# Value sums in two fp32r passes over split pages, finer sample steps, and a new background order in a two-layer decoder step

## The chip, the cores and the metric

One core of a Trainium2 chip runs the whole kernel. The metric is device time in microseconds (us) of one execution. All inputs and outputs are fp32 in HBM.

The engines: TensorE (PE) multiplies, with weight loads shown apart (PEld); VectorE is DVE, ScalarE is ACT, GpSimd is POOL, and SyncE (SP) issues nearly all transfers. Each engine works through its own queue in order.

## The reference, cut to what matters

Two layers over two groups: a prompt (1 x 1024 tokens) and a sample (8 sequences x 8 new tokens behind a past of 1024 tokens in pages of 128). Layer 0 joins a convolution module with stick-breaking attention; layer 1 joins a short convolution with pooling; each is followed by a SwiGLU channel mixer. What the change touches is in layer 0:

```python
proj = hn @ w_in                       # a_val, a_gate, q, k, v
glu = a_val * sigmoid(a_gate)
a = silu(layer_norm(causal_depthwise_conv(ext, conv_w) + conv_b))   # width 31, 512 channels
# stick-breaking attention, 8 heads x 64:
z = einsum('nqhd,nkhd->nhqk', q, k) * scale + bias
log_1m = where(mask, log_sigmoid(-z), 0)
after = cumsum(log_1m, reverse=True) - log_1m
wgt = exp(where(mask, log_sigmoid(z) + after, -inf))
b = einsum('nhqk,nkhd->nqhd', wgt, v)
out = concatenate([a, b]) @ w_out
```

For the sample group k and v come from cache pages named by a page table (8 sequences x 8 pages), with 8 new rows behind them.

## The kernel before, in words

**Operands.** A large product splits weights and activations into a rounded part and a residual (fp32r) and runs three passes (`mm3`, L170). `w_split` (L152 on ACT, L153 on POOL) makes the two halves of a weight tile; three raw and three split tiles rotate. The foreground on PE is such blocks of 24 matmuls or more, one after the other, evacuated by DVE (L226, L230) from two or three accumulators.

**Foreground and background.** The foreground calls a slot function every two of a block's eight steps. In it `bg()` takes one more piece from a generator in `flow`, whose instructions so land between foreground matmuls. A `yield` ends a piece. What is left of a flow when the next stage needs its result is issued by `drain()` without foreground between.

- `flow_ab` runs during the combined input projection `in_proj` of the first half of the prompt (GA, 512 tokens) and of the rest with the sample (GB, 576): `conv_a` (31 taps, 26 of them on DVE with the sum in PSUM, five on ACT and POOL), `conv_norm(GA)`, `attention(GA)`.
- `flow_c` runs during the output projection and the channel mixer of GA: `attention(GB)`, then `conv_b` and `sample()` interleaved, then `conv_norm(GB)`. It is drained in `last_a`, the last out-blocks of the mixer.

**Prompt attention** works by units of one head and 128 queries in four steps, which overlap by one unit each: `s1` scores and two sigmoids (PE, ACT), `s2` scans and product (DVE), `s3` transposes of the weights and their copy `wt` (PE, ACT L826), `s4` value sum (PE L834, in fp32).

**The sample group.** `sample()` goes through 24 units (two sequences together, three key blocks), each in two steps `pr` of two head pairs. `load_k` fetches pages of 128 x 512 into `kst` (six buffers), `trans` transposes them on PE (L922) and splits them (ACT L925, DVE L926) into `kth`, `score` multiplies (L945). A step is three pieces: transposes of the next step's first pair, transposes of its second pair, scores. When two sequences have all scores, `weights`, `weights_b` and `weights_t` follow at fixed step distances (`chain`); `weights_t` transposes nine column blocks in one piece (L994) and copies them (L995). Then 16 value pages are queued in `pvq` and taken two a step: `pv` multiplies 64 weight columns with a page of 128 x 512 in fp32 (L1006), and after eight pages the new rows (L1012). `load_v` brings pages in pairs into two buffers. `conv_b` gets a piece at every second yield of value 2.

**in_proj** for GA starts with the block `first`, in whose middle `norm_a` is issued; `norm_b` (L218) follows the block, and behind it the evacuations.

## Time and profile before

| what | value |
| --- | --- |
| median of 3 runs | 2731.98 us (2730.38 to 2736.82) |
| profiled execution | 2730.78 us, span 2729.0 us |
| PE busy | 2612.9 us, 96% of the span |
| DVE, ACT, POOL busy | 1224.5, 860.4, 1035.5 us |
| HBM read and written | 198.09 and 18.69 MB |
| stage of prompt attention on GB | about 363 to 606 us |
| stage of conv_b and sample | about 606 to 1021 us |

A row of the costliest groups reads: line, engine, operation, tiles written and read, shapes, count, then busy time and mean duration in ns, then the idle time of the engine before such instructions and what ended it. A row of a timeline reads: start, duration, engine, line, operation, count, and in brackets the idle time before it with what ended that. Matmul durations overlap, so the price of one in a stream is the distance from start to start. A row of stretches reads: start and end, length, busy time with count of PE, weight loads, DVE, ACT and POOL, granted clock, DMA share and GB/s.

### The profile page before, as it was taken

The numbers are of one execution on the slowest core, as the hardware profiler recorded it, in microseconds if no ns is written. First come the engines' busy times: TensorE is split into PE (matmuls) and PEld (weight loads), VectorE is DVE, ScalarE is ACT, GpSimd is POOL, SyncE is SP. The second block draws the span as 40 slices with busy tenths as digits, with TensorE's granted clock in tenths as the row PEclk, the third lists the DMA queues.
The fourth block names the chain that finished last, engine by engine and source line by source line (L and its number), as shares of the span: only waits on it lengthen the run. The fifth ranks groups of instructions, "written<-read, shape, count | busy, mean of one in ns | idle before, by whom it ended". The sixth has DMA issues, their size and how long they took to land. (4 is left out here: it accounts for less than half of the span.)

```text
span 2729.0 us, 37771 instructions
## 1 busy us (share of the span) xinstructions
PE 2612.9 (96%) x15423; PEld 2370.5 (87%) x15423; DVE 1224.5 (45%) x1738; ACT 860.4 (32%) x1318; POOL 1035.5 (38%) x589
## 2 busy tenths in 40 slices
PE   7988999899999998899999999999999999999997
PEld 5787877777766656899999989999999999999997
DVE  3775767768777652332222243342222222222226
ACT  4435656653343323242222232123211111111112
POOL 5655233433333327454444452223322222222222
PEclk9999999999999998999999999999999999999999
DMA  6332241124445432422222231131111111111111
GB/s 199 108 102 62 60 114 47 54 64 147 133 132 148 125 116 62 151 78 86 79 85 85 86 99 39 39 100 51 46 44 47 47 40 46 47 43 43 47 39 66
DMA packets 293381, 218.75 MB, mean 80 GB/s; under 512 B 21506, under 2 KB 248962, under 8 KB 293193
## 3 DMA queue, kind: packets, MB, share of 16 engines
q1 hardware_dynamic: 293176, 216.33, 26.6%
q8 instruction: 122, 2.00, 0.3%
q14 instruction: 51, 0.41, 0.0%
q10 hardware_dynamic: 32, 0.01, 0.0%
HBM read 198.09 MB, written 18.69 MB: 79 GB/s over the span
## 5 line engine op out<-in xcount | busy, mean ns | idle before, releaser
L153 POOL TENSOR_TENSOR hl<-stage,hl 128x1024 fp32r<-128x1024 f32 x278 | 683.5, 2461 | 1204.6 <-ACT hl L152 790.0
L170 PE MATMUL acc<-x1t,hl 128*128 128x364 f32 (+1 forms) x4896 | 824.1, 330 | 7.1 <-DVE hb L230 6.4
L170 PEld LDWEIGHTS acc<-x1t,hl 128*128 128x128 f32 x4896 | 817.1, 189 | 9.2 <-ACT x1t L304 6.7
L170 PE MATMUL acc<-x,hl 128*128 128x288 f32 (+1 forms) x4704 | 809.3, 326 | 8.8 <-POOL hl L153 3.2
L170 PEld LDWEIGHTS acc<-x,hl 128*128 128x128 f32 x4704 | 688.2, 189 | 88.8 <-issue 36.0
L170 PE MATMUL acc<-hid,hl 128*128 128x364 f32 (+2 forms) x3024 | 534.5, 335 | 19.9 <-DVE hb L230 15.5
L170 PEld LDWEIGHTS acc<-hid,hl 128*128 128x128 f32 x3024 | 482.2, 191 | 58.5 <-DVE hb L230 20.9
L152 ACT ACTIVATE hl<-stage 128x1024 fp32r<-128x1024 f32 x278 | 291.9, 1053 | 584.3 <-PE acc L170 303.1
L226 DVE TENSOR_TENSOR tmp<-acc,rr 128x728 f32<-128x728 f32 (+2 forms) x230 | 160.8, 721 | 698.1 <-PE acc L170 697.2
L230 DVE TENSOR_TENSOR hb<-acc,hb 128x728 f32<-128x728 f32 (+2 forms) x368 | 255.6, 720 | 280.3 <-PE acc L170 278.9
L176 DVE TENSOR_TENSOR hid<-tmp,hid 128x512 fp32r<-128x512 f32 (+2 forms) x66 | 60.8, 921 | 200.7 <-ACT hid L175 200.7
L187 POOL TENSOR_TENSOR ss<-ss,tmp 128x512 f32<-128x512 f32 (+2 forms) x55 | 97.6, 1774 | 92.9 <-ACT tmp L186 91.9
L175 ACT ACTIVATE hid<-tmp 128x512 fp32r<-128x512 f32 (+2 forms) x66 | 53.5, 810 | 238.4 <-POOL tmp L378 238.3
L378 POOL TENSOR_TENSOR tmp<-tmp 128x512 f32<-128x512 f32 (+2 forms) x66 | 117.0, 1772 | 28.0 <-ACT tmp L366 27.9
L170 PE MATMUL acc<-x1a,hl 128*128 128x512 f32 x480 | 123.0, 410 | 3.4 <-POOL hl L153 2.3
L366 ACT ACTIVATE tmp<-tmp 128x576 f32<-128x576 f32 (+1 forms) x44 | 39.6, 900 | 256.1 <-DVE tmp L226 256.1
L170 PEld LDWEIGHTS acc<-x1a,hl 128*128 128x128 f32 x480 | 90.7, 193 | 27.2 <-POOL hl L153 3.8
L834 PE MATMUL o<-wt,vrow 128*64 128x128 f32 x576 | 78.1, 282 | 16.6 <-ACT wt L826 16.6
L834 PEld LDWEIGHTS o<-wt,vrow 128*64 128x64 f32 x576 | 62.5, 139 | 35.5 <-ACT wt L826 30.3
L688 DVE SCALAR_TENSOR_TENSOR cacc<-ext,par,cacc 128x512 f32<-128x512 f32 x120 | 90.1, 750 | 2.3
L364 POOL TENSOR_TENSOR tmp<-tmp 128x512 f32<-128x512 f32 x22 | 32.4, 1471 | 135.9 <-ACT tmp L363 125.1
L813 DVE TENSOR_TENSOR_SCAN q<-q,ones 128x384 f32<-128x384 f32 (+6 forms) x56 | 77.7, 1388 | 2.0
(222 smaller groups left out, 1898.0 us busy)
## 6 DMA issues: line engine op xcount, KB each, us to landing
stage<-in_w_ffn_in_dram SPq DMA_DIRECT2D x132, 512.0 KB
stage<-in_w_ffn_out_dram SPq DMA_DIRECT2D x66, 512.0 KB
stage<-in_w_in_even_dram SPq DMA_DIRECT2D x40, 512.0 KB
kst<-in_cache_k_dram SPq DMA_DIRECT2D x64, 256.0 KB
vst<-in_cache_v_dram SPq DMA_DIRECT2D x64, 256.0 KB
stage<-in_w_out_even_dram SPq DMA_DIRECT2D x16, 512.0 KB
stage<-in_w_in_odd_dram SPq DMA_DIRECT2D x16, 512.0 KB
park<-hb SPq DMA_DIRECT2D x16, 288.0 KB
```

The costliest lines, as they stand in the source:

```text
L152: act.activation(hl[:, 0], st, AF.Copy)
L153: pool.tensor_tensor(hl[:, 1], st, f32(hl[:, 0]), op=OP.subtract)
L170: pe.matmul(acc[:, b, :c1 - c0], w, x[:, xi, c0:c1], start=first and s == 0, stop=last and s == 2)
L175: act.activation(dst[:, 0], src, AF.Copy)
L176: dve.tensor_tensor(dst[:, 1], src, f32(dst[:, 0]), op=OP.subtract)
L187: pool.tensor_tensor(ss[:, g.cs], ss[:, g.cs], t[:, :g.n], op=OP.add)
L226: dve.tensor_tensor(d, a, r, op=OP.mult)
L230: dve.tensor_tensor(d, a, d, op=OP.add)
L378: pool.tensor_tensor(t[:, :n], t[:, :n], u[:, :n], op=OP.mult)
L688: dve.scalar_tensor_tensor(o, i, w, o, op0=OP.mult, op1=OP.add)
L813: dve.tensor_tensor_scan(e, e, ones[:, 0:1].to_broadcast([128, n - 128]), q[:, n - 128:n - 127], op0=OP.mult, op1=OP.mult)
L834: pe.matmul(o, vrow[h][:, j], w[:, j], start=j == 0, stop=j == i)
```

## The change

It does these things.

1. **Value sums** (`pv`, `weights_t`, `split_v`): each value page is split into rounded part (ACT) and residual (POOL), the weights likewise (ACT, DVE), with the two parts of the weights stacked as 128 columns. A page then is two fp32r matmuls of 128 x 512, and the sum has 128 rows, which `sel` adds up. Raw pages come one by one (`vst`, two buffers of one page); two split pages (`vhl`) are held.
2. **Keys**: transfers of half pages (128 x 256, eight buffers, five ahead); `kth` holds one head pair, in three buffers.
3. **Sample steps**: every piece is a step of its own; the order is transposes of the next step's first pair, scores of this step, transposes of the second pair. `weights_t` goes over three pieces. The distances in `chain` are now in pieces.
4. **Prompt attention**: `s3` comes ahead of `s2` and `s1`; three yields instead of one at the start; two `be` buffers instead of three.
5. **conv_a**: the add that joins the two partial sums is issued eight taps into the next channel; `a2` and `cacc` have two buffers; two yields at the end.
6. **conv_norm**: the scale and shift move from DVE to ACT.
7. **in_proj (GA)**: the second block is issued before `norm_b` and before the first block's evacuation. The first two blocks call no slot inside, the first none behind it either.

```diff
     def conv_a(ep, cp):
...
-            a2 = ep.tile([128, HALF], F, name="a2")
-            acc = cp.tile([128, 512], F, name="cacc")
+            a2 = ep.tile([128, HALF], F, name="a2", bufs=2)
+            acc = cp.tile([128, 512], F, name="cacc", bufs=2)
...
+                if j == OFF + 7 and last:
+                    last.pop()()
...
-            dve.tensor_tensor(a, acc, a2, op=OP.add)
+            last.append(lambda a=a, acc=acc, a2=a2: dve.tensor_tensor(a, acc, a2, op=OP.add))
+        yield 1
+        yield 1
+        last.pop()()
...
-                dve.tensor_scalar(y, y, pc(LNG + c - 1), pc(LNB + c - 1), op0=OP.mult, op1=OP.add)
+                act.activation(y, y, AF.Identity, scale=pc(LNG + c - 1), bias=pc(LNB + c - 1))
...
-                be = bt[u] = pa.tile([128, NKEY], F, name="be", bufs=3)
+                be = bt[u] = pa.tile([128, NKEY], F, name="be", bufs=2)
...
-            yield 1
+            for _ in range(3):
+                yield 1
             for u in range(len(units) + 3):
                 if u >= 3:
                     s4(u - 3)
+                if 2 <= u < len(units) + 2:
+                    s3(u - 2)
                 if 1 <= u < len(units) + 1:
                     s2(u - 1)
...
                     s1(u)
-                if 2 <= u < len(units) + 2:
-                    s3(u - 2)
...
-            KP = 6
+            KP = 5
...
+                    t = kst[j, pr] = sa.tile([128, 256], F, name="kst", bufs=KP + 3)
+                    page_to(t, cache_k[:, :, :, 4 * pr:4 * pr + 4], j)
...
+                    vst[i] = sa.tile([128, 512], F, name="vst", bufs=2)
+                    page_to(vst[i], cache_v, i)
+
+            def split_v(upto):
+                while len(vhl) + vdone[0] < min(upto, 64):
+                    i = len(vhl) + vdone[0]
+                    v = vst.pop(i)
+                    t = vhl[i] = sa.tile([128, 2, 512], FR, name="vhl", bufs=2)
+                    act.activation(t[:, 0], v, AF.Copy)
+                    pool.tensor_tensor(t[:, 1], v, f32(t[:, 0]), op=OP.subtract)
+                    load_v(i + 3)
...
+                t = kth[u, pr, i] = sa.tile([128, 2, 384], FR, name="kth", bufs=3)
...
+                wl = wts[bp] = sa.tile([128, 9, 2, 2, 64], FR, name="wl")
...
-                    act.activation(t[:, c0:c0 + n], m[:, :n * 128].rearrange("p (c r) -> p c r", r=128), AF.Copy)
+                    mv = m[:, :n * 128].rearrange("p (c b r) -> p c b r", b=2, r=64)
+                    o = wl[:, c0:c0 + n]
+                    act.activation(o[:, :, :, 0], mv, AF.Copy)
+                    dve.tensor_tensor(o[:, :, :, 1], mv, f32(o[:, :, :, 0]), op=OP.subtract)
+                    yield
...
-                load_v(i // 2 + 1)
-                pe.matmul(o, wts[bp][:, k, 64 * b2:64 * b2 + 64], vst[i // 2][:, k % 2], start=k == 0, stop=False)
-                if k % 2:
-                    vst.pop(i // 2)
-                    load_v(i // 2 + 3)
+                w = wts[bp][:, :, b2].rearrange("p c s r -> p c (s r)")
+                v = vhl.pop(i)
+                for s in range(2):
+                    pe.matmul(o, w[:, k], v[:, s], start=k == 0 and s == 0, stop=False)
+                vdone[0] += 1
+                split_v(i + 3)
                 if k < 7:
                     return
-                pe.matmul(o, wts[bp][:, 8, 64 * b2:64 * b2 + 64], vnew, start=False, stop=True)
+                for s in range(2):
+                    pe.matmul(o, w[:, 8], vn[:, s], start=False, stop=s == 1)
...
-            while s < len(steps) or chain or pvq or fins:
+            while s < 3 * len(steps) or chain or pvq or fins:
...
+                st, piece = divmod(s, 3)
+                if piece != 1 and st + 1 < len(steps):
+                    trans(*steps[st + 1], piece // 2)
+                if piece == 1 and st < len(steps):
+                    u, pr = steps[st]
                     bp, kb, b2 = units[u]
                     score(u, pr)
...
-                        for d, f in ((1, lambda w=w: next(w)), (2, lambda w=w: next(w)),
-                                     (3, lambda bp=bp: weights_b(bp)), (5, lambda bp=bp: weights_t(bp))):
+                        for d, f in ((2, lambda w=w: next(w)), (3, lambda w=w: next(w)),
+                                     (5, lambda bp=bp: weights_b(bp)), (8, lambda wt=wt: next(wt)),
+                                     (10, lambda wt=wt: next(wt)), (11, lambda wt=wt: next(wt))):
...
-                        chain.setdefault(s + 6, []).append(
+                        chain.setdefault(s + 13, []).append(
...
-                if pvq:
-                    pvq.pop(0)()
+                for _ in range(1 + (st >= len(steps))):
+                    if pvq and (piece != 1 or st >= len(steps)):
+                        pvq.pop(0)()
                 s += 1
-                yield 2
+                yield 1 if todo else 2
...
                 block(g, a, h, x, mid=lambda: box.setdefault("d", norm_a(g, ms, D)))
+                held_back = a
+                continue
+            elif i == first + 1 and first:
+                block(g, a, h, x)
                 norm_b(g, ms, box["d"])
+                evs[first](held_back)
                 evs[i](a)
```

More of the change, by code (lines that the diff above doesn't have):

```diff
@@ L631, in conv_a @@
     def conv_a(ep, cp):
-        g = GA
+        g, last = GA, []
         for c in range(4):
@@ L866, in sample @@
         units = [(bp, kb, b2) for bp in range(4) for kb in range(3) for b2 in range(2)]
-        kpages = [(2 * bp + b2) * 8 + 3 * kb + i for bp, kb, b2 in units for i in range((3, 3, 2)[kb])]
+        khalf = [((2 * bp + b2) * 8 + 3 * kb + i, pr) for bp, kb, b2 in units for pr in range(2)
+                 for i in range((3, 3, 2)[kb])]
         NK = 1032
@@ L914, in trans @@
                 j = (2 * bp + b2) * 8 + 3 * kb
[L915 to L929 removed]
+                load_k(khalf.index((j, pr)) + n)
+                t = kth[u, pr, i] = sa.tile([128, 2, 384], FR, name="kth", bufs=3)
+                m = ms()
+                hp = 2 * pr + i
+                for pg in range(n):
+                    pe.transpose(m[:, pg * 128:pg * 128 + 128], kst[j + pg, pr][:, i * 128:i * 128 + 128], ident)
+                act.activation(t[:, 0, :n * 128], m[:, :n * 128], AF.Copy)
+                dve.tensor_tensor(t[:, 1, :n * 128], m[:, :n * 128], f32(t[:, 0, :n * 128]), op=OP.subtract)
+                if i:
+                    load_k(khalf.index((j, pr)) + n + KP)
+                if kb == 2:
                     b = 2 * bp + b2
[L931 to L933 removed]
+                    new = knew[:, hp, 8 * b:8 * b + 8]
+                    act.activation(t[:, 0, 256:264], new, AF.Copy)
+                    dve.tensor_tensor(t[:, 1, 256:264], new, f32(t[:, 0, 256:264]), op=OP.subtract)
             def score(u, pr):
@@ L938, in score @@
                     z[u] = zp.tile([128, 512], F, name="z")
-                t = kth.pop((u, pr))
                 n = NB[kb]
@@ L942, in score @@
                     hp = 2 * pr + i
+                    t = kth.pop((u, pr, i))
                     q = qb[:, b2, hp * 128:hp * 128 + 128]
                     for s in range(2):
-                        pe.matmul(z[u][:, :n], q, t[:, s, i, :n], start=hp == 0 and s == 0, stop=hp == 3 and s == 1)
+                        pe.matmul(z[u][:, :n], q, t[:, s, :n], start=hp == 0 and s == 0, stop=hp == 3 and s == 1)
             def score_b(u):
@@ L963, in score_b @@
                     act.activation(qf[bp][:, o:o + n], zs[bp][:, :n], AF.Sigmoid, scale=-0.125, bias=brow[:, 1:2])
-            wx, wts, osum = {}, {}, {}
+            wts, osum = {}, {}
             def weights(bp):
@@ L1032, in sample @@
             fill_q(0)
-            load_v(2)
             for _ in range(6):
                 yield 1
+            split(vn, vnew)
+            split_v(1)
+            split_v(2)
             for i in range(2):
```

74 lines of the change are left out of this document (21 added, 53 removed).

## The prediction

> **What bounds the kernel now.** I read the page first, then the profiled execution by stretches, the timeline of TensorE (PE) for its gaps, and the timelines of the engines that end them.
>
> ```profile
> span 2729.0 us, 37771 instructions
> PE 2612.9 (96%) x15423; PEld 2370.5 (87%) x15423; DVE 1224.5 (45%) x1738; ACT 860.4 (32%) x1318; POOL 1035.5 (38%) x589
> 237.00:600.00 363.00, 335.79 (x2042) 280.71 (x2043) 268.43 (x287) 226.52 (x413) 118.77 (x115) 0.98 0.23 64
> 616.00:715.00 99.00, 91.35 (x448) 74.36 (x447) 83.16 (x147) 38.99 (x80) 38.93 (x20) 0.97 0.46 140
> 625.00:1020.00 395.00, 376.21 (x1607) 256.35 (x1605) 283.82 (x502) 139.84 (x286) 125.31 (x65) 0.98 0.44 132
> ```
>
> The last three rows are stretches: start:end, length, then busy time of PE, weight loads, DVE, ACT, POOL. PE has 116 us of idle time in 2729; so the time changes by PE work saved or added and by PE gaps closed or opened. Everything the diff touches lies before about 1100 us. The second cover is thin: in 616 to 715 us DVE is busy 83 of 99 us.
>
> The profiled execution took 2730.78 us (span 2729.0), 1.2 us under the median of the runs, so I carry differences over unchanged.
>
> **Value sums in the steady part (-26.7).**
>
> ```profile
> 732.03 1.07 PE L1006 MATMUL o<-vst,wts 128*64 128x512 f32 x2
> 733.03 1.66 PE L170 MATMUL acc<-hid,hl 128*128 128x512 f32 x6
> 734.53 0.86 PE L945 MATMUL z<-kth,qb 128*128 128x384 f32 x4
> 735.32 1.07 PE L1006 MATMUL o<-vst,wts 128*64 128x512 f32 x2
> 759.42 1.02 PE L1012 MATMUL o<-vnew,wts 128*64 128x512 f32 x2
> 760.37 1.66 PE L170 MATMUL acc<-x,hl 128*128 128x512 f32 x6
> ```
>
> Durations overlap, so I price from start to start. One fp32 page costs 1.00 us (732.03 to 733.03), recorded as two matmuls. Six fp32r matmuls of 512 columns take 1.50 (733.03 to 734.53), 0.25 each, which is one slot of the foreground between two background pieces. The new pv issues two such matmuls: 0.50. Bounds: 0.50 by this row and 1.00 if it gained nothing; I take 0.50, the same type and columns. 48 pages lie in the steady part: 48 x 0.50 = 24.0. The new rows cost 0.95 (759.42 to 760.37), now 0.50: 6 x 0.45 = 2.7. The last 16 pages come below.
>
> **Gaps that the reordering closes.**
>
> ```profile
> 41.94 2.05 PE L218 MATMUL m<-tmp,ones 128*128 128x512 f32 x2 [5.14 <-DVE tmp L209]
> 42.99 10.61 PE L170 MATMUL acc<-x1a,hl 128*128 128x512 f32 x36
> 161.66 1.09 PE L601 MATMUL m<-ident,tmp 128*128 128x128 f32 x4 [6.17 <-DVE tmp L226]
> 237.19 0.50 PE L796 MATMUL z<-kt,qa 128*128 128x512 f32 x1 [3.82 <-ACT qa L778]
> 239.94 0.76 PE L796 MATMUL z<-kt,qz 128*128 128x512 f32 x1 [2.25 <-POOL qz L762]
> 371.47 0.47 PE L796 MATMUL z<-kt,qa 128*128 128x512 f32 x1 [1.50 <-DVE kt L776]
> 372.79 0.47 PE L796 MATMUL z<-kt,qz 128*128 128x512 f32 x1 [0.84 <-DVE qz L779]
> L834 PE MATMUL o<-wt,vrow 128*64 128x128 f32 x576 | 78.1, 282 | 16.6 <-ACT wt L826 16.6
> L825 PE MATMUL m<-ident,be 128*128 128x128 f32 x288 | 42.0, 273 | 0.2 <-DVE be L815 0.2
> 722.11 0.33 PE L994 MATMUL m<-ident,wx 128*128 128x128 f32 x1 [1.83 <-ACT wts L995]
> 815.93 0.33 PE L994 MATMUL m<-ident,wx 128*128 128x128 f32 x1 [2.47 <-ACT wts L995]
> 909.29 0.33 PE L994 MATMUL m<-ident,wx 128*128 128x128 f32 x1 [1.83 <-ACT wts L995]
> 984.18 1.09 PE L994 MATMUL m<-ident,bet 128*128 128x128 f32 x8 [1.94 <-DVE bet L980]
> ```
>
> In in_proj the second block (24 matmuls, 6.0 us) now stands before norm_b and covers the 5.14. The 36 matmuls after that gap take 10.5 us against 36 x 0.25 = 9.0, a slow clock after idling: another 1.5. Together **-6.6**. Two accumulators wait instead of one, of three, so the next block still has one. What is late next is the evacuation after norm_b, with a whole block before its buffer is asked for.
>
> That edit costs four background slots (one of the first block, three of the second), so the convolution starts a block later and leaves less DVE backlog at 161.66. The backlog grows by what eight taps and an evacuation exceed one foreground block, under 1 us: **-0.9** (0 to -2). The deferred add of conv_a stays on DVE and only moves.
>
> Attention on the first half yields three slots instead of one. PE asked for z at 233.4 (237.19 less 3.82) and had both operands at 239.9, 6.1 us of gaps; two more slots (12 matmuls of 288 columns, by scale of the 0.25 some 1.7 us each) cover 3.5 of it: **-3.5** (-6.1 if ACT's Identity, which takes the DVE step out of the chain before it, brings POOL forward; -2 if POOL is simply full). On the second half two slots of 1.5 cover 1.50 and 0.84: **-2.3**.
>
> Moving s3 ahead takes the wt copies out from behind the two sigmoids on ACT and gives them two slots in the second half. The 16.6 us is the whole stake. Against it, the transposes now come sooner after DVE's product: one slot and one s1 earlier, about 2.5 us. They wait 0.2 us in all now, but DVE is busy 268 of 363 us there, and the shorter time leaves several units near zero. Bounds 0 and -16.6; I take two thirds: **-11**.
>
> weights_t in three slots removes the copy that PE waits for inside one piece: 8.07 us in the four rows. Left over is a transpose bank whose DVE subtraction queues behind two taps, about 0.5 us a group: **-6**.
>
> Whether the background still fits is a count of yields in the code. The first flow needed 113 of 121 slots; it now needs 117 of 117 (four lost, two more for conv_a, two for attention) and just fits. The second needed 269 of 280 and now needs 281 (the sample's tail 20 instead of 14, four more for conv_b, two for attention). So the last norm work is issued in the last slot, against the final out-blocks: **+2** (-2 to +8).
>
> **What the change newly asks for.** First the keys:
>
> ```profile
> 685.73 0.38 PE L922 MATMUL m<-ident,kst 128*128 128x128 f32 x2
> 691.47 0.41 DVE L926 TENSOR_TENSOR kth<-m,kth 128x256 fp32r<-128x256 f32 x1
> 694.28 0.66 PE L945 MATMUL z<-kth,qb 128*128 128x264 f32 x4
> L688 DVE SCALAR_TENSOR_TENSOR hb<-ext,par,hb x120: 279/285/2314, 648.8 to 1001.2; 128x64 f32<-128x64 f32 x120
> L688 DVE SCALAR_TENSOR_TENSOR hb<-ext,par,hb 128x64 f32<-128x64 f32 x120 | 57.4, 479 | 3.0
> ```
>
> A score used to follow its transposes by four slots (685.7 to 694.3); now by two, some 4.0 us. Here DVE finishes its residual at 691.9, 6.2 us after: a wait of about 2. This happens where no value pages run and DVE is full, 616 to 715 us; later, with PE slower per step, DVE keeps up. I put **+8** (0 to +15: half of the 16 steps there at 2). On DVE the 120 small taps take 479 ns on average against a median of 285: 23 us lost to something. POOL is busy 125 of 395 us there; 64 more subtractions of about 1.3 us add 83, so by scale 15 us more on DVE, most of it where DVE has room.
>
> The Trainium skill, page "SBUF — State Buffer", section "SBUF: two separate sides", names the cause: VectorE operations with two SBUF inputs and GpSimd operations that read SBUF lock one another out for the whole instruction. The rule speaks against moving splits to POOL. The row agrees (279 at least, 2314 at most).
>
> The half pages double the key transfers on SP, but five half pages lie ahead, so I cost them at nothing; if that cover went, each transfer would show as a PE wait at L922.
>
> Now the value pages. Each goes DMA, ACT copy, POOL subtraction, PE, in two raw and two split buffers; the next load into a raw buffer waits for POOL.
>
> ```profile
> L175 ACT ACTIVATE hid<-tmp 128x512 fp32r<-128x512 f32 x22 | 13.8, 629 | 44.6 <-POOL tmp L378 44.5
> L647 POOL TENSOR_TENSOR a<-a,tapb 128x512 f32<-128x512 f32 x16 | 20.7, 1296 | 0.5
> 988.49 1.99 PE L1006 MATMUL o<-vst,wts 128*64 128x512 f32 x4
> 990.40 1.66 PE L170 MATMUL acc<-hid,hl 128*128 128x512 f32 x6
> 992.00 1.93 PE L1006 MATMUL o<-vst,wts 128*64 128x512 f32 x4
> 991.09 11.24 SPq L419 DMA_DIRECT2D vst<-in_cache_v_dram  x8
> 1007.49 4.08 SPq L419 DMA_DIRECT2D vst<-in_cache_v_dram  x4
> 1011.83 1.93 PE L1006 MATMUL o<-vst,wts 128*64 128x512 f32 x4 [0.62 <-DMA vst<-in_cache_v_dram]
> 0.75 1.83 SPq L489 DMA_DIRECT2D xt<-in_x_prompt_dram  x4
> 3.92 0.47 PE L523 MATMUL m<-ident,xt 128*128 128x128 f32 x1
> ```
>
> A cycle of one buffer: copy 0.63, subtraction 1.30, release to issue 0.7 (990.40 to 991.09), transfer 4.3 (1007.49 to 1011.83) or at most 3.2 (0.75 to 3.92, the same 256 KB); I take 3.6, between, since the tail has few transfers beside it. That is **6.2 us for two pages** (5.8 to 7.0). A steady step asks for two pages every three slots: 4.5 + 0.7 for six transposes (under 685.73's 0.38 for two, as durations overlap) + 0.8 scores (734.53 to 735.32) + 1.0 = 7.0 us. It fits, barely. ACT waits at the split for a landing; queued behind it are the key copies, the gate's copies and the next weight split, and PE would meet that as late keys or weights. SP waits for POOL with the next weights behind it, which are due two blocks later.
>
> In the tail, the last 16 pages come two to a slot. PE alone would need 1.5 + 1.0 = 2.5 us a slot, before it took 3.5 (988.49 to 992.00), or 27.7 for eight. With two slots out of the buffers and six at the cycle: 2 x 2.5 + 6 x 6.2 = 42.2. **+14** (from -8, PE's work alone, to +19).
>
> **Sum.** -26.7 - 6.6 - 0.9 - 3.5 - 2.3 - 11 - 6 + 2 + 8 + 14 = -33. From 2730.8 to 2698 for the execution, and from the median 2732 to **2699**.
>
> **Rivals.**
>
> *The supply keeps up in the tail* (copies, subtractions and transfers overlap more than I chain them): +14 becomes -8, 2677. For it: four buffers. Against: the raw buffer's cycle is a chain.
>
> *DVE becomes the bound in the sample stage.* The two-slot distance costs its 15, the lock adds half of its 15 to PE, and attention gives back five: -33 + 7 + 7 + 5 = -14, 2718. For it: 83 of 99 us busy. Against: over 625 to 1020 us DVE is busy 284 of 395.
>
> *Slower: the value chain binds all along.* POOL takes its queue in order, and the weight split of 2.4 us and the gate's 1.35 stand in it:
>
> ```profile
> L153 POOL TENSOR_TENSOR hl<-stage,hl 128x1024 fp32r<-128x1024 f32 x278 | 683.5, 2461 | 1204.6 <-ACT hl L152 790.0 <-issue 370.4 <-PE m L922 24.0
> ```
>
> With one of these ahead of each subtraction the cycle C is 6.2 + 2.46 + 0.35 = 9.0. Each of three bursts of eight steps then loses 8 x (C - 7.0), less a cushion of about 4 from the filled buffers, and the tail 6 x C + 5 - 27.7. The rest of the sum is -47, so it turns slower from C = 8.3; at 9.0 it gives -47 + 36 + 31 = +20, 2752. Against: the split runs once in four slots, so on average it adds under 1 us.
>
> *The fp32r passes cost what the fp32 ones did*: -33 + 26.7 + 8 = +2, 2734, no change. Against: L170 is fp32r in the same shape at 0.25.
>
> **How the numbers follow.** My forecast, with terms inside their bounds (2685 to 2712): 0.50. Supply keeps up: 0.18. DVE bound: 0.21, of which 0.04 within 0.3%. Value chain all along: 0.09. No gain from fp32r: 0.02. 0.3% is 8.2 us, about what a measurement of this kernel can tell from no change. Faster 0.50 + 0.18 + 0.17 = 0.85; same 0.06; slower 0.09. The range runs from 10 us below the keeping-up case, 2667, to 8 above the DVE case, 2726.
>
> **What would show it.** Right: no wait at L218 near 42 us; L834 waiting under 6 us; two matmuls for each value page, 0.50 from start to start; in the tail, PE waiting on POOL's residual at the value matmuls, some 20 us in all, and slots of about 6 us. Wrong: such waits throughout 730 to 970 us (third rival), score matmuls waiting on DVE by over 15 us (second), or a tail without gaps (first). The forecast falls if POOL's queue holds the splits past 8 us.

## The result, and the profile after

The changed kernel takes 2815.3 us (2814.9 to 2816.2), before 2731.2 in the same comparison (2731.2 to 2733.5 in all comparisons of this study): a ratio of 1.030, 95% interval 1.029 to 1.032. It is slower by 84 us. The forecast was 33 us faster, and the range ended at 2726.

The page of after, its first lines, and one stretch of it (start:end, length, then busy time with count of PE, weight loads, DVE, ACT, POOL, the granted clock, DMA share, GB/s):

```profile
span 2814.5 us, 38562 instructions
PE 2603.7 (93%) x15423; PEld 2405.1 (85%) x15423; DVE 1259.4 (45%) x1759; ACT 907.4 (32%) x1407; POOL 1113.4 (40%) x653
625.00:1020.00 395.00, 302.50 (x1345) 243.10 (x1344) 252.67 (x428) 145.19 (x303) 156.39 (x95) 0.88 0.37 109
```

PE's work is no longer than before (2603.7 against 2612.9 us) but its idle time went from 116 to 211 us. The idle time lies in the sample stage: in the same 395 us PE is busy 302 us rather than 376, at a clock of 0.88 rather than 0.98, while DVE is less busy than before (253 against 284). No engine's busy time fills the stretch; PE waits for something else.

To place the loss, take the same weight splits on POOL in both kernels, the 61st, 105th and 117th of 278. First before, then after, on POOL's timeline:

```profile
590.62 2.54 POOL L153 TENSOR_TENSOR hl<-stage,hl 128x1024 fp32r<-128x1024 f32 x1 [3.82 <-ACT hl L152]
1026.57 2.40 POOL L153 TENSOR_TENSOR hl<-stage,hl 128x1024 fp32r<-128x1024 f32 x1
1118.10 2.49 POOL L153 TENSOR_TENSOR hl<-stage,hl 128x1024 fp32r<-128x1024 f32 x1 [4.16 <-ACT hl L152]
```

```profile
567.30 3.11 POOL L153 TENSOR_TENSOR hl<-stage,hl 128x1024 fp32r<-128x1024 f32 x1 [3.33 <-ACT hl L152]
1091.22 2.39 POOL L153 TENSOR_TENSOR hl<-stage,hl 128x1024 fp32r<-128x1024 f32 x1 [0.15 <-ACT hl L152]
1203.35 2.49 POOL L153 TENSOR_TENSOR hl<-stage,hl 128x1024 fp32r<-128x1024 f32 x1 [4.16 <-issue]
```

By their ends after is 22.8 us ahead at the end of attention (593.16 and 570.41), 64.6 behind near the end of the sample group (1028.97 and 1093.61), 85.3 behind after conv_norm (1120.59 and 1205.84). Nothing changes from there on. So the reordering brought what it should, the sample group lost 87 us, and 21 more went between the 105th and the 117th split, where the group ends and conv_norm runs.

What PE waits for in the sample group is in the groups of page transposes, first before, then after (busy time, mean in ns, then PE's idle time just before and what ended it):

```profile
L922 PE MATMUL m<-ident,kst 128*128 128x128 f32 x256 | 45.2, 280 | 2.0 <-DVE kth L926 1.2 <-ACT wts L995 0.5 <-ACT ext L702 0.3
```

```profile
L940 PE MATMUL m<-ident,kst 128*128 128x128 f32 x256 | 51.3, 290 | 84.1 <-DMA kst<-in_cache_k_dram 70.2
```

Before, the group had 2.0 us of waits and none for a page. One of the waits of after, on the timelines of POOL, SP and PE of after:

```profile
639.91 2.34 POOL L153 TENSOR_TENSOR hl<-stage,hl 128x1024 fp32r<-128x1024 f32 x1 [1.97 <-ACT hl L152]
```

```profile
642.28 0.39 SPq L143 DMA_DIRECT2D stage<-in_w_ffn_in_dram  x1
643.51 3.05 SPq L419 DMA_DIRECT2D kst<-in_cache_k_dram  x3
```

```profile
639.86 0.38 PE L940 MATMUL m<-ident,kst 128*128 128x128 f32 x2
647.13 0.47 PE L940 MATMUL m<-ident,kst 128*128 128x128 f32 x1 [6.89 <-DMA kst<-in_cache_k_dram]
647.67 2.91 PE L170 MATMUL acc<-x,hl 128*128 128x512 f32 x6
```

PE does two of three transposes at 639.9 and stops at the third. Its half page is issued on SP only at 643.5, because SP holds a weight load ahead of it that waits for POOL's split to end (642.25) and free a buffer. With five half pages ahead the third half page of a step is issued one slot before it is used; with the six whole pages of before, the third page of a unit was issued eight slots before. After the wait six matmuls take 2.91 us, where undisturbed ones take 1.65 (the row at 638.38 of the same timeline). The clock granted in those 2.91 us is 0.50:

```profile
647.67:650.58 2.91, 2.91 (x9) 2.33 (x8) 1.98 (x3) 0.76 (x2) 0.00 (x0) 0.50 0.39 110
```

So this long wait costs a second time, through the granted clock. The Trainium skill, page "TensorE: Matmul & The Clock Gate", section "HAM oscillation — how this bites in real kernels", says that an array that idles for a few microseconds is throttled again, so that a loop that waits every round pays the warm-up every round; these rows agree.

### The profile page after: what moved, and what is told of

It is laid out like the page before. It is cut to its first block, busy times and chain, and to the rows that moved or that the text cites. A ratio compares the mean times of both kernels' runs of the same rounds, so it can differ in the third digit from the quotient of the medians.

```text
span 2814.5 us, 38562 instructions
## 1 busy us (share of the span) xinstructions
PE 2603.7 (93%) x15423; PEld 2405.1 (85%) x15423; DVE 1259.4 (45%) x1759; ACT 907.4 (32%) x1407; POOL 1113.4 (40%) x653
## 5 line engine op out<-in xcount | busy, mean ns | idle before, releaser
L170 PE MATMUL acc<-x,hl 128*128 128x288 f32 (+1 forms) x4704 | 818.7, 330 | 12.9 <-DVE hb L230 9.6
L170 PEld LDWEIGHTS acc<-x,hl 128*128 128x128 f32 x4704 | 708.5, 193 | 66.2 <-issue 12.0
L170 PEld LDWEIGHTS acc<-hid,hl 128*128 128x128 f32 x3024 | 488.5, 192 | 41.9 <-DVE hb L230 18.2
L940 PE MATMUL m<-ident,kst 128*128 128x128 f32 x256 | 51.3, 290 | 84.1 <-DMA kst<-in_cache_k_dram 70.2
L940 PEld LDWEIGHTS m<-ident,kst 128*128 128x128 f32 x256 | 35.2, 146 | 104.0 <-DMA kst<-in_cache_k_dram 75.5
L925 POOL TENSOR_TENSOR vhl<-vst,vhl 128x512 fp32r<-128x512 f32 x64 | 81.6, 1283 | 80.4 <-ACT vhl L924 80.4
L942 DVE TENSOR_TENSOR kth<-m,kth 128x384 fp32r<-128x384 f32 (+1 forms) x96 | 48.7, 508 | 89.1 <-ACT kth L941 88.9
```

The source lines that it names most:

```text
L170: pe.matmul(acc[:, b, :c1 - c0], w, x[:, xi, c0:c1], start=first and s == 0, stop=last and s == 2)
L925: pool.tensor_tensor(t[:, 1], v, f32(t[:, 0]), op=OP.subtract)
L940: pe.transpose(m[:, pg * 128:pg * 128 + 128], kst[j + pg, pr][:, i * 128:i * 128 + 128], ident)
```

## The experiments

Theory A: the key lookahead is too short, and SP's order makes it worse. Rivals: the value pages' chain is the limit and the key wait is only where it shows (B); DVE is late with the key splits (C).

**Undo one part at a time.** Four kernels. The first takes the changed kernel and changes a constant:

```
-                    load_k(khalf.index((j, pr)) + n + KP)
+                    load_k(khalf.index((j, pr)) + n + KP + 3)
```

> One constant differs from the changed kernel: a key half page is issued eight ahead of the ones in use rather than five (there are eight buffers in both), so the third half page of a step is issued a full step earlier. Theory A (the changed kernel issues the third half page one slot before its transpose, behind a weight load on SP that waits for POOL's split, and PE waits for it and then runs on at a lower clock): the 146 us of waits on key half pages at the page transposes (70.2 on PE's matmul side, 75.5 on its load side, two records of mostly the same waits) fall below 20 us, the granted clock of the sample stretch rises, and the time falls by 50 to 90 us, to 2725 to 2765 us. Theory B (the splits of the value pages on ACT and POOL are the limit, and the key wait is only where it shows): under 20 us gained, 2795 us or more, with the waits moved to the value products or to other slots. Theory C (PE waits because the transposes and their scores are two slots apart on DVE): under 20 us gained as well, with the waits at the scores.

Measured 2753.4 us (ratio to before 1.0076, 1.0059 to 1.0092): 62 us less by one constant, with no buffer added. I call this the deeper kernel. The second has the sample group of before and all the rest of the change:

> The changed kernel with the sample group as it was before: only the reordering in attention, the first convolution, conv_norm and in_proj is kept. Up to the end of the second attention group the changed kernel was 22.7 us ahead of before by the same weight splits on POOL. Theory A (the loss lies in the sample group's key loading): 2708 us, 23 us under the kernel before, with no loss in the sample stretch; conv_norm of the second group costs what it did before. Rival (the reordering brings the background forward and so onto the sample group at a worse place): 2731 us or more, the 23 us are given back after 600 us.

Measured 2708.6 us (0.9917, 0.9900 to 0.9933), 23.6 under before, and the fastest of all kernels here. The third is the reverse, before with the new sample group:

> The kernel before with the changed kernel's sample group alone (value sums in two passes over split pages and stacked split weights, half pages of keys, thirds of a step): the reordering is left out. Theory A: about 2731 + 87 to 108, 2818 to 2840 us, the whole loss of the change and more. Rival (the loss comes from the two together): under 2790 us.

Measured 2811.9 us (1.0293, 1.0272 to 1.0313): 80 us over before, a little under the stated range. With -23.6 the sum would be 2788, and the change took 2815; 27 us come from the two together. Some 17 of them lie between the 105th and the 117th split (95.0 us in this kernel, 112.2 in the changed one), at the end of the group and in conv_norm; I didn't take them apart further. The fourth takes one page of lookahead from the kernel before:

```
-                    load_k(kpages.index(j) + n + KP)
+                    load_k(kpages.index(j) + n + KP - 1)
```

> The kernel before, with one page less of lookahead: a whole key page is issued five ahead of those in use rather than six, so the last page of a unit of three is issued at the end of the unit ahead of it. Nothing of the change is in it. Theory A (what counts is how few slots lie between the issue of the third page and its transpose, with SP's weight loads ahead of it): slower than before by 10 to 60 us, 2741 to 2791 us, with waits of PE on the key pages at the transposes, where before had next to none. Rival (half pages themselves, twice the transfers on SP, are what costs): 2731 us, no such waits.

Measured 2760.4 us (1.0104, 1.0087 to 1.0121): the same loss in kind, with whole pages and nothing of the change in it. Here the third page of a unit is issued two slots before its use, in the deeper kernel the third half page of a step four slots. The waits of PE (total, times, longest, in us) in the deeper and the shortened kernel, one fence each:

```profile
PE m L940 <- DMA kst<-in_cache_k_dram: 6.0, 5, 2.3
```

```profile
PE m L922 <- DMA kst<-in_cache_k_dram: 20.8, 7, 7.6
```

The 70.2 us fell to 6.0 in the one, and 20.8 arose in the other. By slots of lead the waits are 70.2 us with one, 20.8 with two, 6.0 with four and none with eight. Theory A holds for 62 us of the loss. Theory A expected 2725 to 2765 and got it, yet 2753 is far above the 2699 of the forecast, so something else was wrong too.

**Is it SP's order?** The changed kernel, its lookahead left short, but weight loads in that stage issued by POOL:

```
-            sp.dma_start(stage[i].rearrange("p (k n) -> p k n", k=kt), src)
+            (pool if 58 <= i < 106 else sp).dma_start(stage[i].rearrange("p (k n) -> p k n", k=kt), src)
```

> The changed kernel (2815.3 us) with its short key lookahead as it is, but the weight loads of blocks 58 to 105 issued by POOL's own queue rather than SP's, so that a key transfer on SP stands behind no load that waits for POOL's split. Theory A1 (the hold on SP behind the weight load makes the key pages late): the waits on key half pages at the transposes (70.2 us on PE's matmul side) fall under 30 us, and the time by 30 us or more, to 2785 us or less. Theory A2 (one slot is too short for a transfer in any case, a median of some 2 us and a slot of some 2 us): waits of 1 to 2 us stay at nearly every third transpose, and less than 20 us is gained, 2795 us or more. POOL's issuing may cost something of its own, which would show as its waits on the splits.

Measured 2766.0 us, 49 less. PE's wait on key pages:

```profile
PE m L940 <- DMA kst<-in_cache_k_dram: 12.1, 4, 4.2
```

With no weight load ahead of it on its queue, a page issued one slot early comes in time but for four waits. So the weight load ahead of it makes it late. The run moves that load off SP whole, and so doesn't part its hold from its transfer: of the 6.89 us above, 2.0 pass until SP issues the weight load (640.24 to 642.28), and 4.9 from there until the page has landed. POOL paid 41.1 us of issuing for 48 loads (29.3 and 11.8 in two groups) and the kernel still gained. The Trainium skill, page "Trainium Kernel Development and Optimization", section "Key Constraints", says that issuing from several engines only saves the sequencer's issue time; here it took a load that waits for POOL out of the queue ahead of the pages, so the measurement goes further than the sentence.

**What the value sums cost.** The kernel with the deeper lookahead, with before's value pages, weights and products put back:

> The run with deeper key lookahead (2753.4 us), with its value pages put back to what they were before: whole fp32 products of pairs of pages, unsplit weights, fifteen slots' chain kept. What is left of the change is the reordering, the half pages of keys with eight ahead, and the loop in thirds of a step; the difference to the base is what the two-pass value sums bring or cost, the difference to the run with the reordering alone (2708.6 us) what the new key part costs even with the longer lookahead. By the terms of the prediction (value sums 27 us less in steady state, 14 more in the tail, keys 8 more): about 2753 + 27 - 14 = 2766 us. Rival (the two-pass sums cost more in waits and clock than they save in passes): under 2745 us, faster than its base.

Measured 2727.1 us (0.998, 0.997 to 0.999). So the new key part costs 18.5 over the reordering alone, and the two-pass value sums cost 26.3 more, where the prediction's terms (-26.7 and +14) had them 13 under. The rival expectation was right. Yet PE's saving is there. One undisturbed step of three slots, with whole products, then with two-pass ones, from PE's timelines:

```profile
715.23 0.86 PE L951 MATMUL z<-kth,qb 128*128 128x384 f32 x4
717.75 1.07 PE L1012 MATMUL o<-vst,wts 128*64 128x512 f32 x2
718.76 1.66 PE L170 MATMUL acc<-hid,hl 128*128 128x512 f32 x6
723.17 0.86 PE L951 MATMUL z<-kth,qb 128*128 128x384 f32 x4
```

```profile
718.93 0.86 PE L961 MATMUL z<-kth,qb 128*128 128x384 f32 x4
721.28 0.72 PE L1028 MATMUL o<-vhl,wl 128*128 128x512 f32 x2
721.83 1.56 PE L170 MATMUL acc<-hid,hl 128*128 128x512 f32 x6
725.42 0.86 PE L961 MATMUL z<-kth,qb 128*128 128x384 f32 x4
```

A page goes from 1.01 to 0.55 us, from start to start, and the step from 7.94 to 6.49, 0.73 us a page. To see where this goes, both kernels are cut at the same points of their loops: from the first value product to the last 16 pages, from there to the last value product, and on to the end of the 117th weight split. First with whole products, then with two-pass ones:

```profile
717.75:1001.41 283.66, 269.79 (x1129) 179.13 (x1128) 199.23 (x357) 97.87 (x215) 86.56 (x44) 0.98 0.44 132
1001.41:1034.39 32.98, 30.48 (x88) 12.92 (x87) 11.98 (x18) 4.79 (x9) 8.38 (x5) 0.95 0.45 128
1034.39:1115.44 81.05, 70.45 (x302) 55.15 (x302) 33.38 (x47) 34.20 (x47) 60.17 (x36) 0.96 0.35 110
```

```profile
721.28:1003.13 281.85, 241.57 (x1130) 190.12 (x1129) 209.86 (x346) 122.49 (x261) 147.38 (x92) 0.97 0.44 131
1003.13:1043.77 40.64, 29.40 (x88) 18.30 (x87) 12.40 (x19) 12.00 (x20) 24.67 (x18) 0.83 0.39 116
1043.77:1143.49 99.72, 77.03 (x305) 59.38 (x305) 48.97 (x69) 36.07 (x50) 61.71 (x37) 0.88 0.30 93
```

In the steady part (the first rows) PE works 28 us less, and the stretch is only 1.8 us shorter: PE's idle time goes from 14 to 40 us, while POOL's busy time rises by 61. The last 16 pages take 7.7 us more. The largest part, 18.7 us, is lost behind the last value product, where conv_norm runs. There conv_norm's first sum (L218) stands behind 42 foreground matmuls with whole products and behind 66 with two-pass ones, that is four slots later: `weights_t` in three pieces leaves `conv_b` fewer of its turns. That this lateness is the cause no run shows by itself.

**Who takes it back?** Leave POOL's residuals out, with PE's passes unchanged:

```
-                    pool.tensor_tensor(t[:, 1], v, f32(t[:, 0]), op=OP.subtract)
...
-                    pe.matmul(o, w[:, k], v[:, s], start=k == 0 and s == 0, stop=False)
+                    pe.matmul(o, w[:, k], v[:, 0], start=k == 0 and s == 0, stop=False)
```

> The run with deeper key lookahead (2753.4 us) without POOL's residuals of the value pages: the second pass of each page multiplies the head again, so that the low half of the values is left out of the result; PE's work, ACT's heads and the transfers stay as they are. Theory P (the 64 residuals of 1.27 us on POOL delay the weight splits, SP's loads behind them and the tail's pages, and take back what the shorter value products save): 15 to 26 us less, 2727 to 2738 us. Rival Q (the saving is taken back by DVE and ACT, which are in order and late there: the splits of keys and weights, the convolution): under 10 us less, 2744 us or more, most of it in the tail.

Measured 2727.2 us, 26.2 less: theory P in size. The same three stretches of this kernel:

```profile
717.34:984.40 267.06, 237.98 (x1130) 190.00 (x1129) 196.96 (x347) 123.15 (x261) 87.31 (x44) 0.97 0.47 139
984.40:1019.43 35.03, 24.53 (x88) 17.43 (x87) 11.06 (x20) 12.47 (x21) 7.24 (x4) 0.85 0.45 134
1019.43:1115.11 95.68, 74.52 (x301) 57.41 (x301) 48.13 (x68) 35.51 (x49) 61.24 (x36) 0.89 0.30 95
```

Without residuals the steady part is 14.8 us shorter than with them and 16.6 shorter than with whole products. But PE still idles 29 us there, and behind the last value product 14.6 of the 18.7 us stay lost. That the total equals the kernel with whole products (2727.1) is chance: 16.6 us gained in the steady part, 2.1 and 14.6 lost behind it. Then all residuals on DVE rather than POOL, nothing left out, once on the deeper kernel:

> The run with deeper key lookahead (2753.4 us) with all 64 residuals of the value pages subtracted on DVE rather than on POOL; nothing is left out. Leaving them out brought 26.2 us. If it is POOL's place in the weight splits that they cost (theory P in its narrow form), DVE can carry them: 2728 to 2742 us. If the work itself is what is too much for either engine at the pace of the shortened products (DVE also splits the transposed keys and runs the convolution, and PE waits on it there already), 2748 us or more.

Measured 2749.6 us, 3.8 less than its base, with ranges that touch: the narrow form of P falls. It isn't POOL's place in the order alone; the same work on DVE costs nearly as much. What the residuals do to DVE shows in one group, the 120 small taps of the convolution (busy time, mean in ns, idle before), in the kernels with whole products, with residuals on POOL, without residuals, and with residuals on DVE:

```profile
L693 DVE SCALAR_TENSOR_TENSOR hb<-ext,par,hb 128x64 f32<-128x64 f32 x120 | 57.1, 476 | 3.0
```

```profile
L693 DVE SCALAR_TENSOR_TENSOR hb<-ext,par,hb 128x64 f32<-128x64 f32 x120 | 69.1, 576 | 3.0
```

```profile
L693 DVE SCALAR_TENSOR_TENSOR hb<-ext,par,hb 128x64 f32<-128x64 f32 x120 | 56.2, 468 | 3.0
```

```profile
L693 DVE SCALAR_TENSOR_TENSOR hb<-ext,par,hb 128x64 f32<-128x64 f32 x120 | 59.6, 497 | 3.0
```

With the residuals on POOL the same taps take 12 to 13 us more of DVE (69.1 against 57.1 and 56.2). On DVE the taps are quick again, but DVE carries 53 us of subtractions itself. Either way DVE has less room. These four rows agree with the lock between POOL and two-input DVE operations that the prediction cited. How much of the 26 us goes through DVE, and how much through POOL's weight splits, stays open.

**Small repairs, one each.** All stand on the deeper kernel (2753.4 us). Executions of one kernel here lie up to 9 us apart (2731.4 to 2740.3 us in the widest case), so differences of 3 or 4 us between medians are a sign at most. The first two value pages split later:

```
-            split_v(1)
-            split_v(2)
...
+                if s in (4, 10):
+                    split_v(1 + s // 10)
```

> Base: the run with deeper key lookahead (2753.4 us, 21 over before where the working had 33 under it). Here, in addition, the splits of the first two value pages are issued four and ten slots into the sample group's loop rather than ahead of its first transposes. Theory A (the split on ACT waits for the second value page, which lies behind eight key transfers on SP; ACT's key copies lie behind that split, and PE waits 8.47 us for them at the start of the sample group): that one wait goes, with the stretch of lower clock behind it, 8 to 12 us less, 2741 to 2746 us. Rival (the weights of the filler come late there in any case, since SP holds them behind the same transfers): no change, 2753 us, with PE waiting on the weights in that place.

Measured 2746.7 us, 6.6 less, a little under what was expected; the longest wait of this kind is now 3.1 us. In the changed kernel the chain was visible on SP, ACT and PE:

```profile
593.96 8.64 SPq L419 DMA_DIRECT2D kst<-in_cache_k_dram  x8
603.39 0.34 SPq L419 DMA_DIRECT2D vst<-in_cache_v_dram  x1
```

```profile
606.16 0.63 ACT L924 ACTIVATE vhl<-vst 128x512 fp32r<-128x512 f32 x1 [8.52 <-DMA vst<-in_cache_v_dram]
```

```profile
610.23 0.90 PE L940 MATMUL m<-ident,kst 128*128 128x128 f32 x3 [8.49 <-DVE kth L942]
```

The wait names DVE, but ACT stood still for a value page, and its key copies stood behind that. Scores one slot later (the second transposes move behind them, and the value pages to the other two slots):

```
-                if piece == 1 and st < len(steps):
+                if piece == 2 and st < len(steps):
```

> Base: the run with deeper key lookahead (2753.4 us). Here, in addition, the scores of a step are issued one slot later (three slots behind its second transposes rather than two, five behind its first rather than four). Theory C (the shorter way from transposes to scores costs PE waits on the split of the transposed keys; in that base 8.1 us on the new keys' split, 3.3, 1.2 and 1.1 us on the other splits at the scores, with a lower clock behind each): 12 to 25 us less, 2728 to 2741 us. Rival (DVE as a whole is late there, so that the waits move to the weight transposes and the filler's evacuations): less than 5 us gained.

Measured 2741.2 us, 12.2 less, at the low end, and a new wait came up (21.0 us for the copy of a finished sum, 6.4 in its base), since the gathering products now follow it more closely. Residuals of the last pages on DVE:

```
-                    pool.tensor_tensor(t[:, 1], v, f32(t[:, 0]), op=OP.subtract)
+                    (dve if i >= 48 else pool).tensor_tensor(t[:, 1], v, f32(t[:, 0]), op=OP.subtract)
```

> Base: the run with deeper key lookahead (2753.4 us). Here, in addition, the residuals of the last 16 value pages are subtracted on DVE rather than on POOL. Theory (the tail of the group is paced by POOL: PE waits 8.5 us for the residuals in ten places and 2.5 us for the heads, at a lower clock): 8 to 18 us less, 2735 to 2745 us. Rival (the transfers and ACT's copies pace the tail, a page per about 5 us whoever subtracts; or DVE's convolution work takes the place of POOL): within 4 us of 2753.

Measured 2748.8 us, 4.6 less, between the two; near the rival. The tail's pace, and conv_norm, earlier:

```
+                        ds = (2, 3, 5, 8, 10, 11, 13) if bp < 3 else (1, 2, 3, 5, 5, 5, 6)
...
-                yield 1 if todo else 2
+                yield 1 if todo and st < len(steps) else 2
```

> Base: the run with deeper key lookahead (2753.4 us). Here, in addition, the last chain from scores to value pages is seven slots shorter (its distances 1, 2, 3, 5, 5, 5, 6 rather than 2, 3, 5, 8, 10, 11, 13), and the convolution advances in the tail's slots too, so that conv_norm of the second group comes eight slots earlier: its last work in slot 272 of 280, rather than in 280. Theory (conv_norm's last pieces fall on last_a, where PE waits 7.1 us for the norm's row and 7.4 us for the first prepared operand; the 21.7 us that the base loses between weight blocks 104 and 116 are for half or more that): 10 to 18 us less, 2735 to 2743 us, with those two waits back under 4 us each. Rival (the whole of the 21.7 us is the tail's value pages): 2750 us or more, since the pages come no faster.

Measured 2746.9 us, 6.5 less, between the two expectations. PE's timeline of the base, then of this kernel:

```profile
1102.05 2.39 PE L218 MATMUL m<-tmp,ones 128*128 128x512 f32 x4 [7.11 <-DVE tmp L209]
1113.77 8.67 PE L170 MATMUL acc<-hid,hl 128*128 128x512 f32 x36 [0.43 <-DVE hb L230]
1129.81 10.06 PE L170 MATMUL acc<-hid,hl 128*128 128x512 f32 x30 [7.37 <-DVE hb L230]
```

```profile
1084.44 1.29 PE L218 MATMUL m<-tmp,ones 128*128 128x512 f32 x4 [1.47 <-DVE tmp L209]
1114.27 10.59 PE L170 MATMUL acc<-hid,hl 128*128 128x512 f32 x36 [8.87 <-DVE hb L230]
```

The wait for the norm's row fell from 7.11 to 1.47 us and the one for the first operand (1129.81) is gone, as the theory says. But the 36 matmuls that begin the last output blocks, which waited 0.43, now wait 8.87: on POOL the gate's product stands behind conv_norm's multiplications. The price moved more than it went. All repairs together:

> All single repairs of the run with deeper key lookahead (2753.4 us) together: nine half pages ahead in nine buffers; the first two value pages split later (6.6 us less by itself); scores one slot later (12.2 less); residuals of the last 16 pages on DVE (4.6 less); the shorter last chain with conv_norm eight slots earlier (6.5 less); and, new, the products that gather a finished sample sum come two slots behind its copy rather than one (in the run with later scores PE waits 21.0 us for that copy, in the base 6.4). If the gains add: 2753.4 - 30 - 10 = 2713 us. Theory A, and the prediction's working of the value sums: 2700 to 2720 us. Rival (DVE, ACT and POOL are late as a whole in the sample group, and a wait that is mended turns up in the next place): 2725 us or more.

Measured 2729.9 us, where adding promised 2713: the mended waits turned up elsewhere in part. With all residuals on DVE in that kernel:

> The run with all single repairs (2729.9 us) with all 64 residuals on DVE rather than only the last 16. Narrow theory P: 2710 to 2722 us, near or under the reordering alone (2708.6). If DVE is as full as POOL: 2728 us or more, and then the value sums in two passes bring nothing over whole products in this group, whatever their cover.

Measured 2733.2 us, no gain (2731.4 to 2740.3, its base 2728.0 to 2733.6). In none of the kernels tried did the two-pass value sums beat whole products with the reordering.

**What the key part costs.** Before's value pages, twelve half pages in twelve buffers:

> Base: the run with the key part alone, value pages as before (2727.1 us, 18.5 over the reordering alone). Here with twelve half-page buffers and twelve half pages ahead, as many bytes as the six whole pages before. Theory (what is left of the key part's cost is still lookahead: PE waits 9.1 us for key pages in that base, longest 5.8): 8 to 14 us less, 2713 to 2719 us. Rival (the shorter way from transposes to scores, 5.1, 3.3, 1.2, 1.1 us of waits at the scores in that base, is the rest): under 5 us less, 2722 us or more.

Measured 2718.4 us, 8.7 less than with eight. Nearly all of it lies at the start of the group: by the 68th weight split this kernel is 7.7 us further ahead than at the 64th, and it gains no more after that. One wait of the base is gone here:

```profile
614.47 0.47 PE L930 MATMUL m<-ident,kst 128*128 128x128 f32 x1 [5.79 <-DMA kst<-in_cache_k_dram]
```

From then on eight half pages are as good as twelve. With the scores a slot later and the gathering products two slots behind the copy in addition:

> The run with twelve half pages ahead and value pages as before, and in addition scores one slot later (three slots behind the second transposes, five behind the first; before had three and five too) and the gathering products two slots behind the copy. If lookahead and distance are the whole cost of the key part, it stands within 4 us of the reordering alone, 2705 to 2713 us. If half pages cost by themselves (128 transfers rather than 64 on SP), 2716 us or more.

Measured 2715.3 us: 3.1 more, and 6.7 above the reordering alone, just outside the 4 us that would have closed the account, and close to the 2716 of the other expectation. What is left is the half pages or the new loop; I can't say which.

## Why the prediction was wrong

Bottom up, the steps are: before 2732.2; reordering -23.6; key part with enough buffers and the old distance +6.7, scores and gathering products nearer to what they wait for +3.1, eight half pages rather than twelve +8.7; two-pass value sums +26.3; five half pages ahead rather than eight +61.9; 2815.3. The order matters: each step is measured on top of those ahead of it. The forecast was 116 us away. Of these 62 are the lookahead, 39 the value sums, 10.5 the rest of the key part (18.5 for +8). The 6 us of weights_t don't show as a step: with whole products and the finer steps PE waits 1.9 us for that copy, 6.4 before.

**The step that failed** is "five half pages lie ahead, so I cost them at nothing". It counted buffers, not time: five ahead means that the third half page of a step is issued one slot before its use, and the issue stands on SP behind a weight load that waits for POOL. For the value pages the prediction did see that SP waits for POOL "with the next weights behind it"; it didn't turn this round for the keys, which stand behind the weights. It named what would show it, a PE wait at L922, and this is what came: 70.2 us. The term needed an upper end of its own; one page less of lookahead costs even the kernel before 28 us.

**Value sums, -26.7 and +14.** The price 0.50 a page held (0.55 measured), and so did the tail's length: from the first to the last value product the tail of the changed kernel takes 40.8 us, forecast 42.2.

```profile
1066.54 1.09 PE L1028 MATMUL o<-vhl,wl 128*128 128x512 f32 x4
1106.70 0.63 PE L1034 MATMUL o<-vn,wl 128*128 128x512 f32 x2
1066.50:1107.30 40.80, 28.95 (x88) 18.49 (x87) 12.29 (x18) 11.99 (x20) 24.54 (x18) 0.83 0.39 115
```

That length is partly luck: PE is idle for 11.9 us of it, where the prediction had some 20 of waits on the residual, and the granted clock of 0.83, which had no term, lengthens the rest. What failed is the step from PE's time to the kernel's: of the 28 us that PE saved in the steady part 26 came back as waits. That the 1.0 us products were cover for DVE, ACT and POOL, which the shorter ones cut while the splits added work to the same engines, fits the rows; how much each engine took is not shown. The second rival had the mechanism (the lock, DVE's backlog) but at +14 in all; the value sums cost 26.3 where -12.7 was forecast, 39 us apart. The third rival, slower at 2752, put its waits on the value pages; there PE waited 11.5 us for POOL in all, much less than it needs.

**The reordering, -24.3** without weights_t and conv_norm: measured -23.6. By rows of after, the gap of 5.14 is 0.65, the start of attention on the first half 3.22 for 6.07, and the 16.6 us at L834 (now L839) are gone, but the transposes at L830, moved ahead, wait for DVE instead:

```profile
43.42 1.13 PE L218 MATMUL m<-tmp,ones 128*128 128x512 f32 x2 [0.65 <-DVE tmp L209]
237.82 0.66 PE L801 MATMUL z<-kt,qa 128*128 128x512 f32 x1 [3.22 <-ACT crow L588]
```

```profile
L839 PE MATMUL o<-wt,vrow 128*64 128x128 f32 x576 | 76.6, 278 | 0.4 <-ACT wt L831 0.4
L830 PE MATMUL m<-ident,be 128*128 128x128 f32 x288 | 46.1, 288 | 10.5 <-DVE be L820 9.5 <-ACT tmp L602 0.9
```

Of 16.2 us won there 10.3 were lost to the new wait, net 6 where I took 11. What made up the other 4 us I didn't trace to rows.

**Keys, +8 (0 to +15).** The distance costs 3.1 us where the rest is covered and 12.2 on the kernel with two-pass sums, inside the bounds. But the key part as a whole costs 18.5 even with eight ahead, since 8.7 of it is lookahead once more.

**conv_norm, +2 (-2 to +8).** This term was mis-sized too, if the loss behind the last value product is counted to it: 18.7 us with the two-pass sums, 14.6 without residuals (they lie inside the 39 us above). The prediction had the slots (281 of 280, four of them for conv_b) and priced them at 2. Eight slots more of room, with a shorter tail, brought back only 6.5 in all, so the lateness alone is not shown to be the cause; the reordering alone, two slots later than before, loses nothing there.

## What to carry to other kernels

Count lookahead in time on the queue, not in buffers: ask when the last transfer of a group is issued, in slots before its use, and what stands ahead of it on that queue waiting for another engine. A shorter matmul in a loop that PE shares with three engines is worth its saving only where those engines have the same time to spare; price the cover that goes as well as the passes, and look at the stage behind the loop, where 18.7 of the 26 us lay here. And when one change bundles several, the parts may differ in sign: here the reordering alone (2708.6 us) beats both kernels.

## What was not expected of the hardware

Moving 48 weight loads of 512 KB to POOL's queue took 49 us off the kernel, although each cost 915 or 734 ns of POOL. By contrast, that 64 POOL subtractions of 1.29 us, none of which touch the convolution, lengthened 120 DVE instructions on 64 columns from 468 to 576 ns on average was expected nearly in size: 15 us by the prediction's scaling, 12 to 13 measured.
